# q, k and v computed with features on the partitions, and the rotary rows moved by transfers, in a decoder block on one core

## The chip, the core and the metric

The kernel runs on one core of a Trainium2 chip. The core has TensorE (matrix products, PE in the profile), VectorE (DVE), ScalarE (ACT), GpSimd (POOL) and SyncE (SP). SP, ACT and POOL also issue transfers (DMA), which all run on the core's 16 DMA engines. The engines run side by side and each executes its own instructions in order, waiting on semaphores of the others. The metric is the device time of one execution in microseconds; the median of several runs is compared.

## The reference

One decoder block on x of 1024 tokens and 1024 features, in float32. What bears on the change:

```python
h = _rmsnorm(x, g_mix_pre[l])                       # x * rsqrt(mean(x*x) + eps) * g
proj = einsum('bsd,de->bse', h, w_in[l]) + b_in[l]  # e: 512 pool, 512 q, 128 k, 128 v, 2048 gates
u_pool, q, k, v, gates = split(proj)
q = _partial_rotary(q)    # 8 heads of 64; of each head the first 16 features are turned:
k = _partial_rotary(k)    # 2 heads       t1*cos - t2*sin, t2*cos + t1*sin, with 8 + 8 features
y_attn = _sliding_window_sink_attention(q, k, v, attn_sinks[l])   # blocks of 128 tokens, window 128
```

After that come the gates, the pooling mixer, the output projection, and an MLP of 4096; the change does not touch them.

## The kernel before, in words

**Precision and layout.** Every product is made of three matmuls on a high and a low part of each operand (PASSES: high x high, high x low, low x high). x is loaded transposed (`xt`, features on the partitions), scaled by the gain and split by `scaled` into `xs_[k][th]`: eight slices k of 128 features, two halves th of 512 tokens. The factor of the norm, `r1`, is one number per token: it isn't applied to x but to the results. It comes from `ssq`, the sums of squares of x in rows (`square_row`, ACT), by `rsqrt` (a square root on ACT and small operations on DVE).

**The projection (L180 to L193).** For a block of 128 tokens the piece of x is the stationary operand and the weights move: `mm_q` makes a result of 128 tokens x 512 q features (matmuls of 512 columns), `mm_kv` one of 128 tokens x 256 (k and v). The first loop over k (L216) loads x and the weights and does this for blocks 0 to 3; blocks 4 to 7 are done later. Since tokens are on the partitions of the result, `pre_q` and `pre_kv` close it in one DVE instruction each: times r1 (a per-partition scalar), plus the bias (a row that is broadcast). `rotate` turns the 16 features of all heads (on DVE for block 0, else on GpSimd), and `post_qkv` turns q and k by five transposes on TensorE, since the scores want features on the partitions, and splits them into high and low parts: `qt`, `khi`, `klo`.

**The order.** From L894 on a hand-written program sets the order of TensorE, DVE and ACT; the other queues and, ahead of it, all engines are ordered by the framework. In this program `fill(t)` takes about t us of matmuls from the generator `others`, which yields the projection of the second half, then halves of the gate products. Attention goes block by block: `score_all`, `softmax_max`, `softmax_exp`, `softmax_scale`, `attend_t`, `attend_v`, with a fill between the steps. `make_rb` (L476) writes r1 to DRAM and loads it broadcast over the partitions, `rb`: the gates, whose results have tokens on the free dimension, are multiplied by it later. An accumulator in PSUM is a `bank`: four of tag "mm", two pairs of tag "sc". A tile pool with n buffers makes the n+1st tile of a tag wait until the first is no longer read.

Of the kernel before, what the change touches and what calls it, by code (L numbers as in the profile page):

```python
# [36 lines left out]
C_COS = C_MASK + 2 * P  # L37
C_SIN = C_COS + NT * 8
C_CNT = C_SIN + NT * 8
# [7 lines left out]
V_N = V_ONE + 1  # L47
# [3 lines left out]
def block_kernel(ctx: ExitStack, tc, xt, x, consts, vecs, sinks, b_qkv, g_post, g_mlp, g_mlp_post,  # L51
# [128 lines left out]
    def mm_q(n, k, bq):  # L180
        for j, (xh, h) in enumerate(PASSES):
            pe.matmul(bq, xs_[k][n // 4][:, xh, n % 4 * P:(n % 4 + 1) * P], wq[k][:, h, :],  # L182
                      start=k == 0 and j == 0, stop=k == NK - 1 and j == 2)

    def bkv_of(n):
        return bkv[n // 2 * 2][:, n % 2, :] if n < 4 else bkv[n][:, 0, :]

    def mm_kv(n, k, joint=False):

        for j, (xh, h) in enumerate(PASSES):  # L190
            pe.matmul(bkv_of(n), xs_[k][n // 4][:, xh, n % 4 * P:(n % 4 + 1) * P],  # L191
                      wkv[k // 2][:, h, k % 2, :], start=k == 0 and j == 0 and not (joint and n % 2),
                      stop=k == NK - 1 and j == 2 and not (joint and n % 2 == 0))  # L193

    bq01, bq23 = bank("sc", [2, 512]), bank("sc", [2, 512])
    bq = {0: bq01[:, 0, :], 1: bq01[:, 1, :], 2: bq23[:, 0, :], 3: bq23[:, 1, :]}
    bz = bank("mm")
    bkv = {0: bank("mm", [2, 256]), 2: bank("mm", [2, 256])}
    for j in range(9):
        pe.matmul(bz, zeros[:, :P], zeros, start=j == 0, stop=j == 8)  # L200
    def scaled(t, xs, gk, th, a, b):
        src = xs[:, th * 512 + a:th * 512 + b]
        act.activation(t[:, 0, a:b], src, AF.Identity, scale=gk)
        dve.scalar_tensor_tensor(t[:, 1, a:b], src, gk, f32(t[:, 0, a:b]), ALU.mult, ALU.subtract)


    later = []

    ssq = small()

    def square_row(n):
        t = at(*(("qkv", 3) if n % 2 == 0 else ("s4", 4)), [S])
        nc.sync.dma_start(t, x[n])
        act.activation(t, t, AF.Square, accum_out=ssq[:, n:n + 1])

    for k in range(NK):  # L216
        xs = at("s4", 4, [S])
        ws = stage([768]) if k else ws_first
        if k < 2:
            if k == 0:  # L220
                nc.sync.dma_start(vec, vecs)
            for a, b in ((0, 256), (256, 512)) if k == 0 else ((0, 512),):
                nc.sync.dma_start(xs[:, a:b], xt[k][:, a:b])
            if k:
                nc.sync.dma_start(ws, w_qkv[k])
            else:
                nc.sync.dma_start(ws[:, 512:], w_qkv[k][:, 512:])
            later.append((k, xs))
        else:
            nc.sync.dma_start(xs, xt[k])  # L230
            nc.sync.dma_start(ws, w_qkv[k])
            if k == 2:
                for i, t in later:
                    nc.sync.dma_start(t[:, 512:], xt[i][:, 512:])
        halves_ = [xp.tile([P, 2, 512], F32R, tag="x", name=nm("x")) for _ in range(2)]
        gk = vec[:, V_G + k:V_G + k + 1]
        q = wslot([2, 512]) if k < 6 else ga_.tile([P, 2, 512], F32R, tag="ga", name=nm("wq"))
        if k % 2 == 0:
            wkv.append(ga_.tile([P, 2, 2, 256], F32R, tag="ga", name=nm("wkv")))
        kv = wkv[-1]  # L240
        first = k == 0
        if first:
            split(q[:, 0, :], q[:, 1, :], ws[:, :512], first=dve)
        for a, b in ((0, 256), (256, 512)) if first else ((0, 512),):
            scaled(halves_[0], xs, gk, 0, a, b)
        if not first:
            split(q[:, 0, :], q[:, 1, :], ws[:, :512])
# [2176 lines left out]
```

## Time and profile before

| | |
|---|---|
| time, median of 3 runs | 1087.27 us (1087.07 to 1088.03) |
| the profiled execution's own time | 1087.07 us |
| its span | 1085.3 us |
| TensorE busy | 1076.5 us (99%) |
| DVE / ACT / POOL busy | 892.6 / 635.5 / 102.1 us |
| granted TensorE clock | 0.998 |

A row of the timeline gives the start in us from the span's start, the duration, engine, line, operation, output <- inputs, shapes and the count of instructions merged; in brackets the idle time of the engine ahead of it and what ended that. A row of the chain of waits gives start, length and what ran. A row of the waits reads: engine and line, what it waited for, us in total, times, longest. A row on transfers gives what was written <- read, the issuing queue, the count, KB of one, and the median us from the issue to the landing.

### The profile page before, as it was taken

The page shows a single profiled execution, that of the slowest core. Times are in us where ns is not written, and L with a number is a line of the kernel's source. Part 1 is how long each engine was busy: PE and PEld are TensorE (multiplying, and loading weights), DVE is VectorE, ACT ScalarE, POOL GpSimd, SP SyncE. Part 2 cuts the span into 40 slices and gives each one's busy share as a digit, 9 for nine tenths or more (in the row PEclk, how much of TensorE's full clock was granted, in tenths as well). Part 3 has the DMA queues.
Part 4 walks back from the last instruction along what each step waited for, and adds up shares of the span by engine and source line. Part 5 has one row for each costly group of instructions (what it writes and reads, how often), then busy time and mean ns, then how long its engine had stood idle before and what let it go on. Part 6 is the DMA issues. An engine that isn't in the chain of part 4 may idle for free.

```text
span 1085.3 us, 14915 instructions
## 1 busy us (share of the span) xinstructions
PE 1076.5 (99%) x5355; PEld 907.9 (84%) x5355; DVE 892.6 (82%) x1297; ACT 635.5 (59%) x1058; POOL 102.1 (9%) x174
## 2 busy tenths in 40 slices
PE   9999999999999999999999999999999999999997
PEld 8888888888888888888888888888888898899885
DVE  6688888999787887879979877776757899898997
ACT  6567886466654247587666555555544473275553
POOL 0354311100100012100000000001000000000000
PEclk9999999999999999999999999999999999999999
DMA  9566899679965785822576654656898687469842
GB/s 335 187 188 176 214 248 343 200 240 305 268 212 176 216 203 126 301 83 93 189 256 250 246 203 167 221 184 218 298 385 278 212 273 256 151 183 331 300 132 78
DMA packets 106618, 242.06 MB, mean 223 GB/s; under 512 B 11056, under 2 KB 28592, under 8 KB 106544
## 3 DMA queue, kind: packets, MB, share of 16 engines
q1 hardware_dynamic: 86528, 191.69, 52.1%
q0 software_dynamic: 14112, 29.37, 11.6%
q10 hardware_dynamic: 5904, 20.06, 4.7%
q8 instruction: 42, 0.69, 0.3%
q14 instruction: 32, 0.26, 0.1%
HBM read 166.63 MB, written 73.40 MB: 221 GB/s over the span
## 4 chain that ended last, share of the span: by engine, by line
PE 94%; DVE 2%; ACT 2%; issue 1%; DMA 0%; DVEq 0%; ACTq 0%
PE mm L583 26%; PE at L583 19%; PE at L2129 12%; PE mm L2129 5%; PE mm L1523 5%; PE at L2103 4%; PE mm L2103 4%; PE mm L494 3%; PE sc L182 2%; PE at L1523 2%; PE at L1251 2%; PE mm L191 2%; PE mm L182 2%; PE mm L1251 2%; PE mm L496 1%; PE sc L456 1%
## 5 line engine op out<-in xcount | busy, mean ns | idle before, releaser
L2129 PE MATMUL at<-ar,wh 128*128 128x512 f32 x564 | 134.6, 389 | 0.0
L2129 PEld LDWEIGHTS at<-ar,wh 128*128 128x128 f32 x564 | 105.8, 188 | 22.2 <-DVE ar L104 0.3
L101 ACT CAST wh<-raw 128x1024 fp32r<-128x1024 f32 (+1 forms) x54 | 53.4, 988 | 80.1 <-PE at L2129 52.3
L104 DVE TENSOR_TENSOR wh<-st,wh 128x512 fp32r<-128x512 f32 (+1 forms) x106 | 76.4, 730 | 25.7 <-ACT wh L101 22.1
L583 PE MATMUL mm<-T,wx 128*128 128x512 f32 x375 | 90.6, 389 | 0.0
L104 DVE TENSOR_TENSOR wh<-raw,wh 128x1024 fp32r<-128x1024 f32 (+1 forms) x54 | 61.7, 1142 | 29.9 <-ACT wh L101 29.4
L583 PEld LDWEIGHTS mm<-T,wx 128*128 128x128 f32 x375 | 70.3, 188 | 14.8 <-DVE wx L104 0.2
L101 ACT CAST wh<-st 128x512 fp32r<-128x512 f32 (+2 forms) x105 | 67.6, 653 | 18.8 <-DVE st L539 6.1
L583 PE MATMUL mm<-gr,wh 128*128 128x512 f32 x321 | 77.5, 391 | 0.0
L583 PEld LDWEIGHTS mm<-gr,wh 128*128 128x128 f32 x321 | 59.9, 188 | 12.2
L2129 PE MATMUL mm<-ar,wh 128*128 128x512 f32 x276 | 69.5, 389 | 0.0
L583 PE MATMUL mm<-T,wh 128*128 128x512 f32 x267 | 66.0, 389 | 0.0
L101 ACT CAST ar<-B 128x1024 fp32r<-128x1024 f32 (+2 forms) x59 | 43.0, 757 | 30.7 <-PE mm L2129 14.8
L2129 PEld LDWEIGHTS mm<-ar,wh 128*128 128x128 f32 x276 | 51.8, 188 | 10.8
L583 PE MATMUL at<-gr,wh 128*128 128x512 f32 x243 | 59.0, 389 | 0.0
L583 PE MATMUL mm<-x,wh 128*128 128x512 f32 x240 | 58.8, 394 | 0.0
L583 PEld LDWEIGHTS mm<-T,wh 128*128 128x128 f32 x267 | 50.1, 188 | 10.4
L583 PEld LDWEIGHTS at<-gr,wh 128*128 128x128 f32 x243 | 45.6, 188 | 9.5
L583 PE MATMUL at<-T,wx 128*128 128x512 f32 x213 | 52.2, 389 | 0.0
L583 PEld LDWEIGHTS mm<-x,wh 128*128 128x128 f32 x240 | 44.2, 188 | 9.6 <-ACT f L692 0.2
L104 DVE TENSOR_TENSOR ar<-B,ar 128x1024 fp32r<-128x1024 f32 (+2 forms) x59 | 49.1, 856 | 1.0 <-ACT ar L101 1.0
L2103 PE MATMUL at<-ar,wh 128*128 128x256 f32 x336 | 47.5, 283 | 0.0
(556 smaller groups left out, 2461.0 us busy)
## 6 DMA issues: line engine op xcount, KB each, us to landing
raw<-f_dram SPq DMA_DIRECT2D x40, 512.0 KB, 4.3
B<-in_w_dn_dram SPq DMA_DIRECT2D x32, 512.0 KB, 6.7
st<-in_w_up_dram SPq DMA_DIRECT2D x27, 512.0 KB, 5.2
f_dram<-g SPq DMA_DIRECT2D x21, 512.0 KB, 3.0
wh<-f_dram SPq DMA_DIRECT2D x20, 512.0 KB, 5.1
g<-spill_dram SPq DMA_DIRECT2D x17, 512.0 KB, 5.7
st<-in_w_g_dram SPq DMA_DIRECT2D x16, 512.0 KB, 5.2
f_dram<-g ACTq DMA_DIRECT2D x16, 512.0 KB, 4.1
```

The costliest lines, as they stand in the source:

```text
L101: act.copy(hi, src)
L104: return eng.tensor_tensor(lo, src, f32(hi), ALU.subtract)
L182: pe.matmul(bq, xs_[k][n // 4][:, xh, n % 4 * P:(n % 4 + 1) * P], wq[k][:, h, :], start=k == 0 and j == 0, stop=k == NK - 1 and j == 2)
L191: pe.matmul(bkv_of(n), xs_[k][n // 4][:, xh, n % 4 * P:(n % 4 + 1) * P], wkv[k // 2][:, h, k % 2, :], start=k == 0 and j == 0 and not (joi ...
L456: pe.matmul(yb[:, kv], v[:, c:c + P], p[ph][:, 4 * kv:4 * kv + 4].rearrange("p i q -> p (i q)"), start=j < 2, stop=j >= len(mms) - 2)
L494: pe.matmul(bs[th], whi[:, k, :], rhs(k, hl, th), start=k == 0 and hl == 0, stop=False)
L496: pe.matmul(bs[th], wlo[:, k, :], rhs(k, 0, th), start=False, stop=k == nk - 1)
L583: pe.matmul(b, w[wh][:, kt, :], x_, start=not after and kt == 0 and j == 0, stop=kt == 3 and j == 2, skip_group_check=after)
L1251: pe.matmul(b, w[wh][:, kt, :], xo[xh][:, kt, :], start=not after and kt == 0 and j == 0, stop=kt == 1 and j == 2, skip_group_check=after)
L1523: pe.matmul(bs[t], Am[a][k][ah][:, t * P:(t + 1) * P], Wm[w][k][wh], start=not after and k == 0 and j == 0, stop=k == 3 and j == 2, skip_g ...
L2103: pe.matmul(part[q][:, t, :], o[fs][fh][:, fk, t * P:(t + 1) * P], o[ws][wh][:, wk, :], start=q not in onto and (s_, t, j) == (0, 0, 0), s ...
L2129: pe.matmul(bs[t], fo[fh][:, k2, t * P:(t + 1) * P], wo_[wh][:, k2, :], start=not after and s2 == 0 and k2 == 0 and j == 0, stop=(s2, k2) ...
```

## The change

The weights become the stationary operand, and half of x (512 tokens) moves: `mm_in(f, th, k)` makes a result of 128 features x 512 tokens, for six tiles f of features and two halves th of the tokens. Features are arranged by the host in six tiles: tiles 0 to 3 hold the unturned features of two q heads (48 each) and 32 features of v between them; tiles 4 and 5 hold, in their first 80 partitions, the turned features of all ten heads, each rotary half in the other tile, and in the rest the unturned features of k. So the results already have features on the partitions, and the transposes of q and k go; only v is transposed (`post_v`). What is added:

- The first loop loads and scales only the first half of the tokens; the second half of x is loaded behind the squares of the first four rows. In the first loop matmuls of k = 6 and 7 are done tile by tile, 4 and 5 first.
- `make_rb` is called once for each half of the tokens, from GpSimd's queue, and `close_in` multiplies a tile of results by `rb` (DVE) and adds the bias (ACT, a per-partition scalar).
- `turn` and `turn_end` turn the 80 rows with tables of cos and sin that are loaded (`load_table`), on DVE for the first half, on GpSimd for the second.
- `rows_in`, `keys_rest` and `values_out` move rows between partitions by transfers: turned rows to their place in the tiles of q and k, the unturned rows of k, and the rows of v.
- `split_k` and `split_q` make the high and low parts from SBUF.
- The three fills ahead of the first scores and the softmax, and the places of the later splits, are set anew.

```diff
-    def mm_q(n, k, bq):
-        for j, (xh, h) in enumerate(PASSES):
-            pe.matmul(bq, xs_[k][n // 4][:, xh, n % 4 * P:(n % 4 + 1) * P], wq[k][:, h, :],
...
+    def mm_in(f, th, k, a=0, b=512):
+        for j, (wh, xh) in enumerate(PASSES):
+            pe.matmul(b_in[f, th][:, a:b], w_in_of(f, k, wh), xs_[k][th][:, xh, a:b],
+                      start=k == 0 and j == 0 and a == 0, stop=k == NK - 1 and j == 2)
...
+    def make_rb(th):
+        c, n = slice(th * 512, (th + 1) * 512), slice(4 * th, 4 * th + 4)
+        rsqrt(r1[:, n], ssq[:, n], 4)
+        row = z_dram[0][0][c]
+        nc.gpsimd.dma_start(row.rearrange("(n p) -> p n", p=P), r1[:, n])
+        nc.gpsimd.dma_start(rb[:, c], row.unsqueeze(0).broadcast_to([P, 512]))
...
+        for f in (4, 5, 0, 1, 2, 3):
+            for k in (6, 7):
+                mm_in(f, 0, k)
+        for n in range(4):
+            square_row(n, at("qkv", 3, [S]) if n < 3 else at("s4", 4, [S]))
+        make_rb(0)
+        load_table(0)
+        for k in range(NK):
+            if k % 2 == 0:
+                xs = flat(yy.tile([P, 2, 512], F32, tag="y", name=nm("xs")))
+            nc.sync.dma_start(xs[:, k % 2 * 512:(k % 2 + 1) * 512], xt[k][:, 512:])
+            scaled(k, 1, xs[:, k % 2 * 512:(k % 2 + 1) * 512])
+        for n in range(4, NT):
+            square_row(n, at("s8", 3, [2, 4, P]).rearrange("p a b k -> p (a b k)") if n < 7 else at("s4", 4, [S]))
...
-    def pre_q(n):
-        dve.scalar_tensor_tensor(tf_of(n)[:, :512], bq[n], r1[:, n:n + 1], bq_b[:, :512], ALU.mult, ALU.add)
...
+    def close_in(f, th):
+        raw_in(f, th)
+        t = raw_of(f, th)
+        dve.tensor_tensor(t, b_in.pop((f, th)), rb[:, th * 512:(th + 1) * 512], ALU.mult)
+        act.activation(t, t, AF.Identity, bias=vec[:, V_BQ + f:V_BQ + f + 1])
...
+    def turn(th, eng):
+        t, tab = raw_r[th][:NR], tables.pop(th)
+        turned[th] = [at("s4", 4, [2, 512])[:NR] for _ in range(2)]
+        for i, o in enumerate(turned[th]):
+            eng.tensor_tensor(o, t, tab[:NR, i, :].unsqueeze(1).broadcast_to([NR, 2, 512]), ALU.mult)
+
+    def turn_end(th, eng):
+        t, (a, b) = raw_r[th][:NR], turned.pop(th)
+        eng.tensor_tensor(t[:, 0], a[:, 0], b[:, 1], ALU.subtract)
+        eng.tensor_tensor(t[:, 1], a[:, 1], b[:, 0], ALU.add)
+
+    MOVES = ((0, 0, 16, 56), (1, 0, 8, 48), (1, 8, 16, 72))
+
+    def rows_in(q, th, dst, m):
+        for i, a, b, to in MOVES:
+            q.dma_start(dst[to:to + b - a], raw_r[th][16 * m + a:16 * m + b, i, :])
+
+    def split_k(th):
+        c = slice(th * 512, (th + 1) * 512)
+        split(khi[:, c], klo[:, c], raw_k.pop(th))
...
     def others():
+        for f in (4, 5, 0, 1, 2, 3):
+            b_in[f, 1] = bank("mm")
+            for k in range(NK):
+                mm_in(f, 1, k)
...
+                if k == NK - 1:
+                    close_in(f, 1)
+                    if f == 5:
+                        keys_rest(nc.sync, 1)
+                        turn(1, pool)
+                        turn_end(1, pool)
+                        rows_in(nc.sync, 1, raw_k[1], 4)
+                    elif f < 4:
+                        values_out(nc.sync, 1, f)
+                        rows_in(nc.sync, 1, raw_of(f, 1), f)
+                    if f == 1:
+                        split_k(1)
                 yield 3 * 0.227
...
-        rsqrt(r1, ssq[:, :NT], NT)
-        make_rb()
...
+        close_in(4, 0)
+        close_in(5, 0)
+        turn(0, dve)
+        keys_rest(nc.sync, 0)
+        load_table(1)
+        for m in (0, 1):
+            close_in(m, 0)
+            values_out(nc.scalar, 0, m)
+        make_rb(1)
+        turn_end(0, dve)
+        rows_in(nc.sync, 0, raw_k[0], 4)
+        for m in (2, 3):
+            close_in(m, 0)
+            values_out(nc.scalar, 0, m)
...
-        fill(5.7)
...
+        fill(5.4)
+        split_k(0)
+        split_q(0)
+        fill(3.4)
         score_all(0)
```

**Where the order shows it.** First TensorE ahead of the scores of block 0 (`sc<-klo,qt`). Before, these rows stand there (`mm_529` is the kv result of block 4, `mm_596` the q result of block 5):

```order
L191 MATMUL mm_529<-wkv_365,x_363 128x256 x3
L191 MATMUL mm_529<-wkv_365,x_406 128x256 x3
L182 MATMUL mm_596<-wh_120,x_119 128x512 [waits DVE_49]
L182 MATMUL mm_596<-wh_120,x_119 128x512 x2
L388 MATMUL sc_601<-klo_470,qt_558 128x128 [waits DVE_49]
```

In the changed kernel (`mm_555` is tile 5 of the second half; tile 4 of the second half, `mm_520`, is complete ahead of these rows):

```order
L185 MATMUL mm_555<-x_124,wkv_118 128x512 [waits PE_49]
L185 MATMUL mm_555<-x_124,wkv_118 128x512 x2
L185 MATMUL mm_555<-x_168,wkv_118 128x512 x3
L185 MATMUL mm_555<-x_200,wkv_195 128x512 x3
L185 MATMUL mm_555<-x_230,wkv_195 128x512 x3
L185 MATMUL mm_555<-x_262,wkv_257 128x512 x3
L420 MATMUL sc_572<-klo_457,qt_550 128x128 [waits DVE_49,PE_49,Activation_49]
```

The transposes are gone, and the first scores come behind 24 + 15 matmuls of the second half.

Second, DVE ahead of the splitting of k (`klo`) of block 0. Before, the rows are these, and `r_86` (r1) is what the closing instructions read:

```order
L311 SCALAR_TENSOR_TENSOR qkv_490<-sc_98,r_86,bc_460 128x512
L311 SCALAR_TENSOR_TENSOR tf_492<-sc_99,r_86,bc_460 128x512
L311 SCALAR_TENSOR_TENSOR tf_494<-sc_99,r_86,bc_460 128x512
L104 TENSOR_TENSOR qt_558<-mm_551,qt_558 128x512 [waits Activation_49]
L104 TENSOR_TENSOR klo_470<-mm_552,khi_469 128x128 [waits Activation_49]
```

In the changed kernel they read `rb_all`, and the closing of tile 4 of the second half (`mm_520`) stands ahead of `klo`. Its waits hold DMASW3, the fourth transfer of GpSimd's queue, which is the load of the second half of rb:

```order
L346 TENSOR_TENSOR qkv_460<-s_69_465,s_70_466 80x512
L347 TENSOR_TENSOR qkv_460<-s_69_465,s_70_466 80x512
L332 TENSOR_TENSOR qkv_499<-sc_99,rb_all 128x512 [waits PE_49]
L332 TENSOR_TENSOR qkv_499<-sc_99,rb_all 128x512
L941 TENSOR_SCALAR nsnk<-snk 128x8 [waits DMAHW5_49]
L332 TENSOR_TENSOR qkv_545<-mm_520,rb_all 128x512 [waits DMAHW3_49,DMAHW2_49,DMAHW4_49,DMAHW1_49,DMAHW5_49,DMAHW0_49,DMAHW6_49,DMASW3_49,DMAHW7_49,DVE_49,PE_49]
L103 TENSOR_TENSOR klo_457<-s_71_469,khi_456 128x512 [waits Activation_49]
L103 TENSOR_TENSOR qt_550<-qkv_474,qt_550 128x256 [waits Activation_49]
```

So k and q of the first half are split behind a wait for the factor of the second half.

Third, ACT from the first bias (L333, of tile 4 of the first half, which needs rb of that half) to the square root of the second half (`sm_481<-ssq`, L108):

```order
L333 ACTIVATE qkv_460<-qkv_460,vec 128x512 [waits DVE_49]
L207 ACTIVATE s_60_435,ssq<-s_60_435 128x1024 [waits DMAHW0_49]
L333 ACTIVATE qkv_460<-qkv_460,vec 128x512 [waits DVE_49]
L207 ACTIVATE s_61_438,ssq<-s_61_438 128x1024 [waits DMAHW1_49]
L207 ACTIVATE s_62_441,ssq<-s_62_441 128x1024 [waits DMAHW2_49]
L207 ACTIVATE s_63_444,ssq<-s_63_444 128x1024 [waits DMAHW3_49]
L333 ACTIVATE qkv_474<-qkv_474,vec 128x512 [waits DVE_49]
L362 DMA tv<-qkv_474 32x512 [waits Activation_49]
L333 ACTIVATE qkv_474<-qkv_474,vec 128x512 [waits DVE_49]
L362 DMA tv<-qkv_474 32x512 [waits DMAHW4_49,Activation_49]
L108 ACTIVATE sm_481<-ssq,eps 128x4
```

Before, the eight squares and one square root of all tokens stood together ahead of every closing; now the squares of rows 4 to 7 are behind the first closings.

266 lines of the change are left out of this document (117 added, 149 removed).

## The prediction

> **What bounds the kernel now.** I read the busy times first, then the chain that ended last, then TensorE's own waits, and then the first 70 us (the only stretch that the change touches) instruction by instruction.
>
> ```profile
> PE 1076.5 (99%) x5355; PEld 907.9 (84%) x5355; DVE 892.6 (82%) x1297; ACT 635.5 (59%) x1058; POOL 102.1 (9%) x174
> PE 94%; DVE 2%; ACT 2%; issue 1%; DMA 0%; DVEq 0%; ACTq 0%
> ...
> PE mm L200 <- PEq L2410: 0.8, 1, 0.8
> PE sc L431 <- DVE s L420: 0.2, 1, 0.2
> ```
>
> TensorE works from the first microsecond to the tail and makes up 94% of the chain; in the whole span it waits for others 1.0 us. So a matmul less is time won, and every new microsecond in which TensorE must wait is time lost, one for one. The stretch of the change in the chain of waits:
>
> ```profile
> 0.78 4.18 PE mm L200 x9
> 4.95 3.41 PE sc L182 x12
> ...
> 34.90 2.75 PE sc L182 x12
> 39.08 5.47 PE mm L182 x24
> 45.44 2.51 PE mm L191 x21
> 48.65 1.49 PE sc L388 x24
> ```
>
> A matmul of 512 columns costs 5.47/24 = 0.228 us, one of 256 columns 2.51/21 = 0.1195, and the first k is 3.41 - 2.75 = 0.66 us late. The first scores (L388) start at 48.65, with no gap ahead of them.
>
> **TensorE's work.** The kv matmuls (L191) are 192 of 256 columns, 22.9 us; the change has 96 more of 512 in their place, 21.9: 1.0 saved. The first k's twelve 512-wide ones become 24 of 256: 12 x (0.239 - 0.228) = 0.13 lost. Of 40 transposes (five a block) 8 stay:
>
> ```profile
> 58.43 0.60 PE L344 MATMUL mm<-cst,tf 128*128 128x128 f32 x4
> 58.87 0.27 PE L345 MATMUL mm<-cst,tf 128*128 128x128 f32 x1
> ```
>
> Four take 58.87 - 58.43 = 0.44 from start to start, 0.11 each; 32 fewer save 3.5. In sum TensorE has 4.4 us less to do. That is the whole possible gain.
>
> **What the first scores wait for.** In the kernel before, the factor r1 (one value per token) is a per-partition scalar: once it is in SBUF, the projections are closed. Its copy along the free dimension, rb, is made too, but nobody wants it before the gates. Now that tokens lie on the free dimension, closing a tile needs rb: for each half of the tokens r1 goes to DRAM in elements of 4 bytes and comes back broadcast. This is the same pair of transfers that the profile shows off the path:
>
> ```profile
> 35.84 1.06 ACT L214 ACTIVATE s<-s 128x1024 f32<-128x1024 f32 x1 [0.16 <-DMA s<-in_x_dram]
> 37.01 1.28 ACT L109 ACT_TABLE_LOAD   x1
> 39.48 0.17 DVE L121 TENSOR_TENSOR r<-sm,sm 128x8 f32<-128x8 f32 x1
> 39.68 0.37 SPq L479 DMA_DIRECT2D spill_dram<-r  x1
> 50.03 0.34 SPq L480 DMA_DIRECT2D rb_all<-spill_dram  x1
> ...
> spill_dram<-r SPq DMA_DIRECT2D x1, 4.0 KB, 10.3
> rb_all<-spill_dram SPq DMA_DIRECT2D x1, 512.0 KB, 4.8
> spill_dram<-st SPq DMA_DIRECT2D x8, 256.0 KB, 2.4
> f<-spill_dram POOLq DMA_DIRECT2D x5, 256.0 KB, 3.8
> g<-spill_dram POOLq DMA_DIRECT2D x3, 256.0 KB, 6.2
> ```
>
> 4 KB took 10.3 us to land where 256 KB took 2.4, and the load behind it really waited: it was issued at 50.03. The packet counts of two stretches (40.4 to 41.0 and 41.0 to 41.6) say why it is not the engines' work:
>
> ```profile
> DMA packets 649, 0.00 MB, mean 4 GB/s; under 512 B 649, under 2 KB 649, under 8 KB 649
> ...
> DMA packets 386, 0.00 MB, mean 3 GB/s; under 512 B 386, under 2 KB 386, under 8 KB 386
> ```
>
> The 1024 elements had left by 41.6, and the landing came 8.4 us later: something behind the engines takes about 8 ns for each. The change writes 512 at a time, from GpSimd's queue, whose small writes this trace does not show. Low bound: 2.4, as a plain write. High: 10.3, as now. I take the row it is nearest to, with half of what goes with the count: 2.4 + (10.3 - 2.4)/2 = 6.4. For the load of 256 KB the rows on GpSimd's queue give 3.8 to 6.2; I take 5.0 for the first (the second half of x is still being loaded then) and 3.8 for the second.
>
> **When each happens.** The loads ahead of the last square were 8 x 896 KB + 8 x 512 KB = 11.5 MB before, landing at 35.84 from about 2.5: 0.346 MB/us. Ahead of the fourth square are now 8 x 640 KB + 4 x 512 KB = 7.3 MB: 2.5 + 21.2 = 23.7. From that landing to r1 the kernel before took 39.65 - 35.84 = 3.8, so the first half of r1 is there at 27.5, and rb at R = 27.5 + 6.4 + 5.0 = 38.9. Two of the tiles to be closed will have been done on TensorE since about 33.
>
> The second half's r1 stands behind R, because ACT executes in order: the bias of tile 4 (which needs rb) is ahead of the squares of tokens 4 to 7, and these are ahead of the second square root. Prices:
>
> ```profile
> 27.15 1.34 ACT L203 ACTIVATE x<-s,vec 128x512 fp32r<-128x512 f32 x2
> ...
> 45.91 1.40 DVE L311 SCALAR_TENSOR_TENSOR tf<-sc,r,bc 128x512 f32<-128x512 f32 x2
> 47.22 0.68 DVE L104 TENSOR_TENSOR qt<-mm,qt 128x512 fp32r<-128x512 f32 x1
> 61.73 1.32 DVE L420 TENSOR_TENSOR s<-s,den 128x1024 f32<-128x1024 f32 x1
> ```
>
> Closing tile 4 on DVE 0.65, two x pieces queued behind it 1.3, closing tile 5 0.65, its bias on ACT 0.7: R + 3.3. ACT then has three squares of 1.24 (1.06 and the accumulator's read), to R + 7.0, while DVE turns (two of 1.2) and closes tiles 0 and 1, also to R + 7.0; then two biases (0.67) with a DMA issue of 0.4 behind each, R + 9.1, the root 0.3 and four dependent small operations on DVE 1.2: r1's second half at R + 10.6. Its round trip is 6.4 + 3.8, so all of rb is there at R + 20.8. The rows that are put in place meanwhile (some twenty transfers of 16 to 96 KB, 0.4 us of issue each on SP and ACT, 2 to 3 us to land) leave from R + 11.9 and are there by about R + 19: hidden by that second trip; without that cover they cost what they take after it, up to their own 7 us.
>
> Why should the scores of block 0, which are of the first half, wait for the second half's rb? Because closing tile 4 of the second half is written ahead of the splitting of k and q in DVE's order, and its bias ahead of the casts in ACT's. DVE stands at that instruction, and queued behind it are klo, both pieces of q's low part, presum and the first softmax; PE waits for them at the first scores. After rb: closing 0.65, bias 0.67, the cast of k 0.6, low part of k and the first piece of q 1.0: the scores start at R + 23.7 = 62.6.
>
> TensorE is there much earlier: 4.95 + 0.66 + 24 x 0.1195 + 132 x 0.228 = 38.6 for the first half, and 39 matmuls of the second, 8.9: **47.5**. It stops for 62.6 - 47.5 = **15.1 us**. Bounds: with 2.4 and 3.8 on both trips 27.5 + 6.2 + 10.6 + 6.2 + 2.9 = 53.4, a stop of 5.9; with 10.3 and 6.2 it is 74.0, a stop of 26.5.
>
> After a stop TensorE may start slowly. The nearest row is the span's own start: nine matmuls of 512 columns took 4.18 us, where 9 x 0.228 = 2.05 would do, so 2.1 lost; bounds 0 and 2.1, and I take 2.1, since a stop of 15 us is more like a start than like a gap. [...]
>
> Later only one place worries me. The second half is turned on GpSimd, and its prices there are:
>
> ```profile
> 66.94 0.54 POOL L326 TENSOR_TENSOR rb<-qkv,cst 128x160 f32<-128x160 f32 x1
> 69.01 0.35 POOL L328 TENSOR_TENSOR qkv<-qkv,rb 128x80 f32<-128x80 f32 x1
> 72.95 0.98 POOL L326 TENSOR_TENSOR rb<-qkv,cst 128x160 f32<-128x160 f32 x1
> ```
>
> 0.19 us for 80 elements more: 2.5 for 1024 and 1.3 for 512, 7.6 for the four, and up to 14 where they run as slowly as the 0.98. If T is the start of the first scores, key tile 5 is closed and biased at T + 7, turned at T + 14.6 to 21, in place 3 us later; ACT's cast of those keys is ahead of its copy that frees a bank for the scores of block 2, which TensorE reaches at T + 22.3. With cast and copy (1.6) that is a stop of 0 to 3.3; I take 1.5. DVE's extra work (twelve closings of 0.65, two turns of 1.2, for twelve closings of 0.7 and 0.45) and ACT's twelve biases lie in the stop or beside TensorE's fill work: nothing; without that cover ACT's are 8 us.
>
> **Sum**, against the profiled execution's own 1087.07 us (0.2 from the median 1087.27, so the same): 1087.1 - 4.4 + 15.1 + 2.1 + 1.5 = 1101.4, said as 1101.
>
> **The rivals.** (1) *Small transfers at their floor.* If 512 elements from GpSimd's queue land as fast as the quickest rows of the trace, the trips are short:
>
> ```profile
> out_dram<-xf SPq DMA_DIRECT2D x6, 256.0 KB, 2.1
> st<-wbp_dram SPq DMA_DIRECT2D x8, 256.0 KB, 2.9
> ```
>
> Two trips of 2.1 + 2.9: 27.5 + 5.0 + 10.6 + 5.0 + 2.9 = 51.0, a stop of 3.5, 1086. Against it is the 10.3. [...] (2) *Faster*: rb is never late, as the first half's loads are fewer, and TensorE runs through: 1087.1 - 4.4 = 1082.7. For it speaks that TensorE never waited for x before. It needs both trips together within 47.5 - 27.5 - 10.6 - 2.9 = 6.5 us, four landings of 1.6 where the quickest is 2.1; or r1 some microseconds earlier. (3) *More stops*: the first trip is stretched by the loads of x (10.3 instead of 6.4 for the write), and the turn on GpSimd runs at its slow price: 1101.4 + 3.9 + 1.2 (6.2 for that load, too) + 1.8 = 1108.
>
> **How the numbers follow.** Forecast 0.67, with a range of its own of 1094 to 1107; rival 1 0.10, rival 2 0.06, rival 3 0.17. The bounds of the stop without any other loss give 1087.1 - 4.4 + 5.9 = 1088.6, and with all 1087.1 - 4.4 + 26.5 + 2.1 + 3.3 = 1114.6; the range is 1088 to 1114. What a measurement can tell is 0.2%, 2.2 us: rival 2 and part of rival 1 are faster (0.08), most of the rest of rival 1 is the same (0.07), the others are slower (0.85).
>
> **What would show it.** In the changed kernel's profile: a stop of TensorE of about 15 us ahead of the first scores (L420), near 47; DVE's L332 waiting about ten us for the load of rb_all; two writes of r, 2 KB each, at 5 to 8 us; TensorE's work 4 us less. Wrong would be writes of r at 2 to 3 us, r1's first half well before 25, or no stop at the scores. If the stop is there and the time is still near 1087, work that I take as fixed was saved later.

## The result, and the profile after

The changed kernel takes **1141.54 us** (median of four runs, 1141.02 to 1143.64) beside 1087.17 for the kernel before in the same session: a ratio of 1.0503, 95% interval 1.0490 to 1.0516. It is slower, as forecast, but by 54 us and not by 14, and the time lies above the forecast's range (1088 to 1114). The profiled execution took 1141.17 us, its span is 1139.0, the granted clock 0.981 (0.998 before).

TensorE's busy time and its waits in the changed kernel (engine and line, what it waited for, us in total, times, longest):

```profile
PE 1096.9 (96%) x5239; PEld 905.4 (79%) x5239; DVE 899.3 (79%) x1301; ACT 644.5 (57%) x1081; POOL 97.2 (9%) x146
```
```profile
PE sc L420 <- DVE klo L103: 21.7, 1, 21.7
PE mm L185 <- DVE x L201: 7.2, 1, 7.2
PE sc L420 <- ACT yt L490: 2.5, 2, 2.2
PE sc L463 <- DVE s L429: 1.0, 2, 0.5
PE sc L463 <- DVE s L452: 1.0, 1, 1.0
PE mm L196 <- PEq L2457: 0.8, 1, 0.8
```

The stop ahead of the first scores is there (L420), and a second one that the prediction did not have: the second half's x pieces (L201) stand on DVE behind the closing of tile 4, which waits for rb. The chain of waits and DVE's two waits at the closing (L332):

```profile
31.85 12.32 DMA spill_dram<-r
...
44.47 4.58 DMA rb_all<-spill_dram
...
52.51 3.12 ACT s L207 x6
...
62.17 6.63 DMA tv<-qkv
68.82 4.90 DMA qkv<-qkv
...
74.43 1.98 DMA qkv<-qkv
...
79.51 2.85 PE sc L420 x24
...
82.76 6.54 PE mm L185 x21
```
```profile
49.14 0.69 DVE L332 TENSOR_TENSOR qkv<-mm,rb_all 128x512 f32<-128x512 f32 x1 [13.64 <-DMA rb_all<-spill_dram]
...
76.68 0.69 DVE L332 TENSOR_TENSOR qkv<-mm,rb_all 128x512 f32<-128x512 f32 x1 [14.63 <-DMA qkv<-qkv]
```

rb's first half was there at 49.1. What ended DVE's second wait is not the second half of rb but the moved rows (`qkv<-qkv`): they have to be out of a buffer that the second half takes over. The two writes of r1 on GpSimd's queue, of 2 KB each, landed 12.3 and 8.1 us after their issue:

```profile
spill_dram<-r POOLq DMA_DIRECT2D x1, 2.0 KB, 12.3
...
spill_dram<-r POOLq DMA_DIRECT2D x1, 2.0 KB, 8.1
```

The table by stretches gives for each the length, the busy time of PE, PEld (weight loads), DVE, ACT and POOL with counts, the granted clock, the share of the DMA engines' time, and GB/s. It shows a half clock up to about 86, seven us after TensorE had gone back to work (0.68 is 6.4 us at a half), and once more behind a stop of only 2.2 us at 108 to 110:

```profile
70.00:80.00 10.00, 0.49 (x4) 0.52 (x6) 2.02 (x5) 3.33 (x6) 0.00 (x0) 0.50 0.23 57
80.00:90.00 10.00, 10.00 (x56) 8.26 (x58) 7.01 (x13) 3.93 (x13) 2.98 (x3) 0.68 0.25 81
...
108.00:110.00 2.00, 0.04 (x2) 0.04 (x2) 0.96 (x2) 2.00 (x4) 0.00 (x0) 1.00 0.51 158
110.00:112.00 2.00, 2.00 (x14) 1.68 (x15) 1.66 (x3) 0.98 (x2) 0.00 (x0) 0.57 0.34 64
```

And a loss that no wait shows. From about 200 us on both kernels run the same code, and yet the distance between them grows: the gates begin at 162.35 before and 201.82 after (39.5 later), the MLP's 384 matmuls end at 865.95 and 918.75 (52.8 later). The granted clock is 1.0 in both. The groups of matmuls say where; a row ends with the count, the busy us, the mean ns of one, and the idle time ahead:

```profile
L2167 PE MATMUL at<-ar,wh 128*128 128x512 f32 x564 | 138.8, 396 | 0.0
...
L607 PE MATMUL mm<-T,wx 128*128 128x512 f32 x375 | 90.7, 389 | 0.0
```
```profile
L2129 PE MATMUL at<-ar,wh 128*128 128x512 f32 x564 | 134.6, 389 | 0.0
...
L583 PE MATMUL mm<-T,wx 128*128 128x512 f32 x375 | 90.6, 389 | 0.0
```

The second fence is the kernel before. The same 564 matmuls take 396 ns instead of 389, while others kept their 389.

### The profile page after: what moved, and what is told of

The parts are those of the page before. It is cut to its first block, busy times and chain, and to the rows that moved or that the text cites. A ratio compares the mean times of both kernels' runs of the same rounds, so it can differ in the third digit from the quotient of the medians.

```text
span 1139.0 us, 14784 instructions
## 1 busy us (share of the span) xinstructions
PE 1096.9 (96%) x5239; PEld 905.4 (79%) x5239; DVE 899.3 (79%) x1301; ACT 644.5 (57%) x1081; POOL 97.2 (9%) x146
## 4 chain that ended last, share of the span: by engine, by line
PE 85%; DMA 5%; ACT 4%; DVE 4%; issue 1%; SPq 0%; ACTq 0%; DVEq 0%
PE mm L607 25%; PE at L607 18%; PE at L2167 12%; PE mm L2167 5%; PE mm L1561 5%; PE at L2141 3%; PE mm L2141 3%; PE mm L518 3%; PE at L1561 2%; PE at L1289 2%; PE mm L1289 1%; PE mm L520 1%; DMA spill_dram<-r 1%; PE sc L420 1%; DMA s<-in_x_dram 1%
## 5 line engine op out<-in xcount | busy, mean ns | idle before, releaser
L2167 PE MATMUL at<-ar,wh 128*128 128x512 f32 x564 | 138.8, 396 | 0.0
L607 PEld LDWEIGHTS mm<-T,wx 128*128 128x128 f32 x375 | 70.4, 188 | 14.9
L607 PE MATMUL at<-gr,wh 128*128 128x512 f32 x243 | 60.8, 396 | 0.0
L100 ACT CAST ar<-B 128x1024 fp32r<-128x1024 f32 (+2 forms) x59 | 43.0, 756 | 30.0 <-PE mm L2167 15.2
L607 PEld LDWEIGHTS mm<-T,wh 128*128 128x128 f32 x267 | 50.2, 188 | 10.9
L607 PE MATMUL at<-ar,wh 128*128 128x512 f32 x192 | 47.5, 396 | 0.0
```

The lines of the kernel that those rows point to most:

```text
L100: act.copy(hi, src)
L607: pe.matmul(b, w[wh][:, kt, :], x_, start=not after and kt == 0 and j == 0, stop=kt == 3 and j == 2, skip_group_check=after)
L2167: pe.matmul(bs[t], fo[fh][:, k2, t * P:(t + 1) * P], wo_[wh][:, k2, :], start=not after and s2 == 0 and k2 == 0 and j == 0, stop=(s2, k2) ...
```

## The experiments

All times stand beside a kernel before of 1087.1 to 1087.9 us in the same session. Line numbers of the variants are one to some ten lines higher than in the changed kernel.

### Where the operands lie in SBUF

The slow groups are those with an operand in the buffers `ga` or `g` (names `ar`, `gr`). The change dropped the tables of cos and sin and a tile of `rotate`, so these buffers begin elsewhere. First bytes of the buffers modulo 256, as the built programs place them:

```
               weights (wh)   ga, g (ar, gr)   x, wx, yp, most of T
before             224             224             224
after              224             128             224
```

**a_shift96**, the changed kernel:

```diff
     pad = sp.tile([P, 32], F32, name="pad", bufs=1)
+    dve.memset(sp.tile([P, 24], F32, name="gap", bufs=1), 0.0)
```

> The changed kernel with one unused tile of 96 bytes per partition ahead of the big buffers and nothing else. In the changed kernel some tiles were dropped and made smaller, so the buffers that hold operands of the later stages (tags ga and g) begin at an address that is 0 modulo 128, where it was 96 before; the weights (tag wh) and x stay at 96. Theory: the place of the operands in SBUF costs the matmuls their 2 to 3% (the MLP's 384 matmuls 87.04 us before, 89.96 after). Then the last 940 us get some 14 us back: 1127, and those 384 matmuls take 87. Rival: the slower matmuls are an after-effect of the stops (a clock or power state); then nothing moves: 1141, 90.

Measured: 1127.76 us (1126.84 to 1130.9), 13.8 less; the MLP's 384 matmuls take 87.04 us again, and the 564 above 389 ns.

**b_shift32**, **b_shift64**, **b_shift128**: the kernel before with such a tile of 32, 64, 128 bytes. **b_all0**: 32 bytes ahead of all big buffers and 96 on the right side, where x lies.

> The kernel before with an unused tile of 32 bytes per partition, which puts the buffers ga and g at 0 modulo 128, as in the changed kernel, and nothing else. By the theory of the place it loses what the changed kernel lost after 200 us, 14 to 16 us: about 1102, and the MLP's 384 matmuls take 90. By the rival: 1087, 87.

> The kernel before with an unused tile of 64 bytes, so that ga and g begin at 32 modulo 128, which is 32 modulo 64 as before. If what counts is the place modulo 64, nothing moves: 1087, 87. If it is the place modulo 128 against that of the other operand (96), it loses as the shift by 32 does: 1102, 90. If the stops are the cause: 1087.

> The kernel before with 32 bytes ahead of all big buffers on the left and 96 on the right, so that every operand begins at 0 modulo 128. If what costs is that the two operands lie differently, nothing is lost: 1087, 87. If an operand at 0 modulo 64 is slow by itself, the loss is that of the shift by 32 or larger, since x and the weights have it too: 1102 to 1115, 90. If the stops are the cause: 1087.

> The kernel before with an unused tile of 128 bytes ahead of the buffers ga and g. In all runs so far the matmuls ran at 389 ns where both operands begin at the same place modulo 256, and at 391 to 396 where they do not. If 256 is the measure, this run is slow as the shift by 32 is: 1097 to 1102, ar against wh 391 to 396. If 128 is the measure, nothing moves: 1087, 389.

Measured: 1101.33 us for 32 bytes (ratio 1.0131, 1.0116 to 1.0146), 1096.67 for 64 (1.0085, 1.0070 to 1.0100), 1101.97 for 128 (one run), 1097.81 for b_all0 (1.0098, 1.0081 to 1.0115). So an unused tile of 32 bytes makes the kernel before 14 us slower. Which groups, in three fences (32 bytes; 128 bytes; b_all0):

```profile
L2130 PE MATMUL at<-ar,wh 128*128 128x512 f32 x564 | 138.2, 395 | 0.0
```
```profile
L2130 PE MATMUL at<-ar,wh 128*128 128x512 f32 x564 | 138.1, 395 | 0.0
```
```profile
L2132 PE MATMUL at<-ar,wh 128*128 128x512 f32 x564 | 134.6, 389 | 0.0
...
L586 PE MATMUL at<-x,wh 128*128 128x512 f32 x96 | 23.6, 394 | 0.0
```

In b_all0 `ar` begins at the very byte at which it is slow with 32 bytes (50432), and is fast, because the weights now begin at 0 modulo 256 too; x, at 128, is slow instead. So the place of one operand does not count, but that of the two against each other: the large groups at 389 ns have both at the same place modulo 256, and a difference of 32, 64 or 128 costs 2 to 7 ns of each matmul. Modulo 64 and modulo 128 are excluded as the measure by the 64 and the 128 bytes. More than 256 is not needed: in the kernel before, `wh` begins at 24032, `ar` at 50400 and `yp` at 147424, an odd and an even multiple of 256 away, and both pairs run at 389. Equal places are not the whole of it: behind 200 us, 36 of that kernel's 44 groups of this shape run at 389, the others at 390 to 399. Why the chip does so stays open. Of the change's 54 us, 14 are this. It comes with the tiles that were dropped, not with the layout of q, k and v or its stops.

### What the first scores wait for

**a_order**, on a_shift96:

```diff
-        fill(5.4)
         split_k(0)
         split_q(0)
-        fill(3.4)
+        fill(8.8)
```

> The changed kernel with the 96 bytes (1127.8), and the splitting of k and q of the first half moved ahead of the first fill, so that on DVE and ACT it no longer stands behind the closing of tile 4 of the second half, which reads the second half of rb. The prediction's step: this order alone makes the first scores wait for the second half's factor; then they start when the first half is ready and most of the stop of 22.6 us goes: 1110 or less. Rival, from the trace of the changed kernel: the last to land ahead of the scores are the moved rows of q of the first half (77.0; rb's second half is there at 73.8), which the scores need in any order; then only the closing and bias that stood ahead go (0.7 + 0.7): 1126.

Measured: 1127.89 us (1125.75 to 1129.87): nothing. The order that the prediction blamed is there, but it isn't what ends last.

**a_norows**, on a_order: the twelve `rows_in` of q's first half left out.

> The kernel of a_order (splits ahead of the fill, 1127.9, no gain), with the twelve transfers left out that put the turned rows of q's first half in place (the output lacks them; the rows of k and v are still moved). If the row moves are what the first scores wait for, the splitting of k and q can start when the rows of k are there, some 4 us after the end of the turn at 60.7, and the scores 2 to 3 us later, at 67 instead of 80: 1115. If they wait for something else (the second half's factor, the biases), the scores stay at 77 or later: 1125 or more.

Measured: 1120.29 us (1118.24 to 1120.94), 7.6 less. The stop fell from the first row (a_order) to the second (a_norows), and the third, from the chain of a_norows, says what holds it now:

```profile
PE sc L421 <- DVE klo L103: 21.0, 1, 21.0
```
```profile
PE sc L421 <- DVE klo L103: 13.2, 1, 13.2
```
```profile
62.64 8.00 DMA s<-qkv
```

The moved rows of q were last, as the rival said. But the rows of k, 64 KB in three transfers, now take 8.0 us by themselves, not the 4 I had put down. They land at 70.6, and the second write of r1, issued at 60.9, lands 9.3 us later, at 70.2: the rows wait about as long as that write is under way.

**a_rbpe**, on a_shift96, takes both trips away:

```diff
-        row = z_dram[0][0][c]
-        nc.gpsimd.dma_start(row.rearrange("(n p) -> p n", p=P), r1[:, n])
-        nc.gpsimd.dma_start(rb[:, c], row.unsqueeze(0).broadcast_to([P, 512]))
...
+        diag = tv[:, c].rearrange("p (n q) -> p n q", q=P)
+        dve.tensor_tensor(diag, ident.unsqueeze(1).broadcast_to([P, 4, P]),
+                          r1[:, n].unsqueeze(2).broadcast_to([P, 4, P]), ALU.mult)
+        b = bank("mm")
+        pe.matmul(b, ones, tv[:, c], start=True, stop=True)
+        act.copy(rb[:, c], b)
...
```

> The changed kernel, with both round trips of r1 through DRAM taken out: the factor is put on a diagonal (DVE, 128 x 512) and TensorE multiplies it by a matrix of ones, which puts r1 along the free dimension in all partitions; ACT copies that to rb. Two f32 matmuls of 512 columns more, the constants are loaded ahead of the second half of x, the big buffers lie as with the 96 bytes (1127.8). rb's first half should then be there at about 34.5 instead of 49.1, and r1's second half 10.4 later, at 45. If the trips are the whole cause, as predicted, and the moved rows take 7 us, the first scores start at about 55, TensorE stops some 4 us there and nowhere before: 1101. If the moves take what they took in the changed kernel (16 us from the end of the turn at 46), they become the bound: scores at 64, a stop of 11 to 13: 1109. If the trips are not the cause: 1127.

Measured: **1108.05 us** (1103.71 to 1110.27; ratio 1.0174, 1.0147 to 1.0202), 19.7 less than a_shift96. rb's first half is copied at 35.2. What is left:

```profile
PE mm L224 <- DVE tv L222: 6.5, 1, 6.5
PE sc L428 <- DVE klo L103: 3.3, 1, 3.3
PE sc L428 <- ACT yt L498: 3.2, 3, 2.3
```

The first is the multiplication for the second half, which stands too early in TensorE's order; the second is the stop at the scores. All its waits but the one at the start come to 18.0 us; one minus the clock, by what TensorE was busy in each stretch of 10 us, to 6.5. Less the 2.6 of saved work that are left (4.4, less an estimated 1.8 for the two f32 matmuls), that is 21.9 of the 23.2 us by which the profiled run lies above the kernel before.

From its chain, the first transfer of the values that ends a wait, and the last moved row:

```profile
49.90 1.99 DMA tv<-qkv
...
55.71 1.99 DMA qkv<-qkv
```

The turn ends at 48.5 and the last moved row lands at 57.7: 9.2 us. In the changed kernel the same moves take from 60.8 to 76.4, 15.6 us. Of the 6.4 more, 4.6 are in the transfer of the values (6.63 instead of 1.99), which lands 0.7 behind the write of r1 that was issued ahead of it; the rest comes behind it, while the second half of rb is loaded. Both are gone in a_rbpe, so this run alone doesn't tell them apart; in a_norows the rows of k were held before that load was issued, at 70.4.

### What a small write costs, and whom

**a_writes**, on a_shift96: five more writes on GpSimd's queue.

```diff
+    def write_rows(t):
+        nc.gpsimd.dma_start(scrap[:512].rearrange("(n p) -> n p", p=P), t)
+
+    def write_elements(t, n):
+        nc.gpsimd.dma_start(scrap[:n * P].rearrange("(n p) -> p n", p=P), t)
+
+    write_rows(gap[:4, :P])
+    write_elements(gap[:, P:P + 1], 1)
+    write_elements(gap[:, P:P + 4], 4)
...
+        write_rows(rb[:4, 512:640])
+        write_elements(r1[:, 4:5], 1)
```

> The changed kernel with five more writes on GpSimd's queue, each behind the landing of the one ahead, to a row of DRAM that nobody reads: while the loads run, 4 rows of 512 bytes, 128 elements of 4 bytes, 512 elements of 4 bytes; and behind the second load of rb, in a quiet stretch, the 4 rows and 128 elements again. By the prediction's step (a fixed price, and a part that goes with the number of elements) in the quiet: rows 2.4, 128 elements 3.4, and 512, which the kernel itself writes, 6.4 (measured: 8.0 to 8.5). If the loads stretch a write as they did for the first factor (11.8 to 12.6): 512 elements 10 or more, and the rows, being four packets, at most 4.

Measured, in the order of issue: the rows, 128 elements, 512 elements, all under the loads; then rows and 128 elements again in the quiet:

```profile
spill_dram<-gap POOLq DMA_DIRECT2D x1, 2.0 KB, 2.7
...
spill_dram<-gap POOLq DMA_DIRECT2D x1, 0.5 KB, 10.5
...
spill_dram<-gap POOLq DMA_DIRECT2D x1, 2.0 KB, 10.1
...
spill_dram<-rb_all POOLq DMA_DIRECT2D x1, 2.0 KB, 1.8
...
spill_dram<-r POOLq DMA_DIRECT2D x1, 0.5 KB, 8.2
```

The number of elements is not the price: 128 cost 8.2 us, 512 cost 8.1 to 9.3 behind the loads, 1024 cost 10.3 in the kernel before. That it is elements of 4 bytes is: the same 2 KB in rows of 512 bytes take 1.8. And others pay too. Two stretches of a_writes, the first with a write of elements under way, the second with none (last columns: share of the DMA engines' time, GB/s), and the first of them in a_shift96:

```profile
20.00:24.00 4.00, 4.00 (x19) 3.30 (x19) 0.97 (x2) 0.18 (x1) 0.00 (x0) 1.00 1.13 68
...
28.00:32.00 4.00, 4.00 (x19) 3.34 (x18) 1.54 (x3) 1.94 (x4) 0.00 (x0) 1.00 1.04 414
```
```profile
20.00:24.00 4.00, 4.00 (x20) 3.30 (x19) 1.86 (x4) 2.81 (x6) 0.00 (x0) 1.00 1.02 408
```

The engines are busy and move 68 GB/s instead of 408. It isn't so for the whole of a write: in stretches of 1 us the loads run on at first, and then stay at 34 to 105 GB/s (from 11 to 17, and from 20 to 27; the two writes were issued at 4.4 and 15.2). Two such writes during the loads made r1's own write start at 42.1 instead of 31.1, and the one run came out at 1137.1 us, 9.3 more. So an element write holds up loads, as the rows of k in a_norows and the values in the changed kernel were held up beside one.

**a_rows**, on a_shift96 (constants loaded early as in a_rbpe): `pe.transpose(b[:4, :P], r1[:, n], ident)`, a copy on ACT, and a write of 4 rows.

> The changed kernel with the 96 bytes (1127.8), and r1 written to DRAM in rows: TensorE transposes the 128 x 4 values to 4 x 128, ACT copies them, and GpSimd's queue writes 4 rows of 512 bytes in place of 512 elements; the broadcast load stays. In a_writes such rows landed in 1.8 to 2.7 us, the elements in 8.2 to 10.9. If the 4-byte elements are the price, each write falls by 6 to 9 us: rb's first half at 42 instead of 49, r1's second half at 52, the scores at 63 to 65 (moved rows last): 1110 to 1113. If any write of that queue pays it, nothing moves: 1127.

Measured: 1124.99 us (1123.01 to 1126.71): only 2.8 less, where I had expected 15 or more. The price of the write fell (6.2 in place of 12.4 under the loads, and 1.6 in place of 8.1 behind them), but the scores start at 75.9, only 3.9 earlier:

```profile
PE mm L221 <- DVE r L120: 13.4, 1, 13.4
PE sc L428 <- DVE klo L103: 12.4, 1, 12.4
```

The second transpose stands in TensorE's order ahead of 18 matmuls and waits there for r1, and ACT's copy of its result stands behind ACT's six moved rows: it ran at 67.1, though r1 was there at 56.7. rb's first half came at 46.2 (49.1). The moved rows, with no write under way, take 9.1 us here (the turn ends at 57.9, the last lands at 67.0), as in a_rbpe. So this run shows the price of the elements, what it does to the moved rows, and that a cheap trip in a bad place of an in-order queue wins nothing; it says nothing on what a well placed one would give.

### The cold clock

**a_warm**, **a_warm2**, **a_warm3**, on a_shift96: matmuls of zeros added to the accumulation of tile 5 of the second half: 85 ahead of k = 7 in a_warm, 85 ahead of k = 4 in a_warm2, 100 there in a_warm3, which the diff shows.

```diff
+                if f == 5 and k == 4:
+                    for j in range(100):
+                        pe.matmul(b_in[f, 1], zeros[:, :P], zeros, start=False, stop=False)
```

> The changed kernel with the 96 bytes, and 85 matmuls of zeros (19.3 us) added to the accumulation of tile 5 of the second half, ahead of its last k, so that TensorE is busy in the stop. They end ahead of the first scores, so the stop itself stays. If a cold clock costs what the trace shows (the granted clock is a half from 62 to 86, and the scores' matmuls run at half rate to 86.4), it comes back: the clock stays 1.0 from 56 on, and 3.5 us are won: 1124. If ACT and DVE set the pace there anyhow, nothing: 1128.

> As a_warm, with the 85 matmuls of zeros ahead of k = 4 of tile 5 of the second half, which TensorE reaches before the first scores (in a_warm they stood ahead of k = 7, which it reaches only behind them, so they cost their own 18.6 us). They fill the stop from about 57 to 77; the scores still start at 80. If the cold clock costs, 3 to 3.5 us come back: 1124; if DVE and ACT set the pace anyhow, nothing: 1128.

> As a_warm2 (1128.1), with 100 instead of 85 matmuls of zeros, so that they reach the first scores (a_warm2's ended 3.7 us ahead of them, and the clock fell to a half again in that gap: 0.73 from 80 to 90). If the half clock costs what the trace shows behind the stop, about 3.5 us come back: 1124.5. If DVE and ACT set the pace there, nothing: 1128.

Measured: 1149.63, 1128.1 and 1127.1 us. In a_warm the filler stood behind the first scores, so it only added time (21.9 us, for 85 matmuls that are an estimated 19.3). In a_warm2 it ended 3.7 us early, and the clock fell again in that gap. In a_warm3 it reached the scores (the rows are a_warm2 and a_warm3):

```profile
80.00:90.00 10.00, 10.00 (x64) 8.46 (x66) 7.23 (x14) 3.98 (x14) 3.26 (x3) 0.73 0.27 88
```
```profile
80.00:90.00 10.00, 10.00 (x63) 8.10 (x62) 7.54 (x13) 6.95 (x27) 5.87 (x4) 1.00 0.48 149
```

The gates then start at 199.3 instead of 202.5: 3.2 us won, as expected. In the whole time the gain is 0.7, within the 4 us by which the runs of these variants differ; in the profiled run 2.6 us were lost again between 600 and 620, where TensorE waited for a cast of weights. So the size of the loss is shown where it arises, and not in the whole.

### The layout without its stops

**a_best** and **a_best2**, on a_rbpe: the turn of the first half ahead of the second square root, rows moved from three queues (in a_best2 from SP's and GpSimd's), a fourth buffer for the raw results, more matmuls ahead of the first scores; in a_best2 the second half is turned on DVE too. In a_best the values leave behind the rows that take their place, so v holds turned rows there; number and size of the transfers are those of a_best2.

> The layout of the change with every cause taken out that the runs have shown: buffers at the same place modulo 256, rb made by TensorE, DVE's turn of the first half not behind the second square root, the second half's factor needed only behind the split of k and q, rows moved from three queues, a fourth buffer for the raw results, and 14.3 us of the second half's matmuls ahead of the first scores instead of 8.8. If stops, clock and matmul pitch were the whole loss, what is left is the forecast without stops, 1087.1 - 4.4, plus two f32 matmuls (1.8) and some 3 us of the small stops in the softmax: 1087 to 1090. If the layout costs something else that I have not seen: 1095 or more.

> As a_best, with what its trace showed mended: the second half is turned on DVE, behind the first block's softmax (GpSimd's turn made two copies on DVE take 2.8 us each instead of 0.73); the row moves of the second half leave from GpSimd's queue, so that no load of weights stands behind them on SP's; the values go out ahead of the rows that take their place (in a_best behind them, so that its values were overwritten); 12.2 us of matmuls ahead of the first scores. TensorE then arrives at 52, the moved rows land at about 54 and the scores start at 56: a stop of 4, a cold clock of 3 behind it, 3 us of small stops: 1087.1 - 4.4 + 1.8 + 10 = 1094. If the layout costs something unseen: 1105 or more.

Measured: 1118.01 (1115.9 to 1118.95) and 1115.83 us (1114.34 to 1117.12), both slower than a_rbpe. The stop ahead of the first scores is gone in a_best, and 3.3 + 0.9 us in a_best2 (ahead of the multiplication for rb, and of the scores), but new ones came. In a_best (DVE, then GpSimd):

```profile
59.20 5.68 DVE L441 COPY_PREDICATED s<-cst,pad 128x512 f32<-128x512 uint32 x2
```
```profile
58.78 5.52 POOL L354 TENSOR_TENSOR s<-qkv,s 80x1024 f32<-80x1024 f32 x2 [2.24 <-ACT qkv L345]
```

Two copies that take 0.73 us each elsewhere (a_rbpe, at 63.2) end at 64.9, just behind the first two instructions of GpSimd's turn (64.3), and a wait of 4.3 us at the scores of block 1 follows. The two rows show them side by side; why the copies are slow then, no run here shows. In a_best2 waits of 0.3 to 3.3 us remain, 18 us in sum; the longest, and two stretches:

```profile
PE mm L228 <- DVE tv L222: 3.3, 1, 3.3
PE mm L619 <- ACT wh L100: 2.0, 1, 2.0
```
```profile
90.00:100.00 10.00, 8.53 (x39) 6.98 (x39) 6.68 (x9) 6.13 (x23) 5.09 (x11) 0.73 0.82 211
100.00:110.00 10.00, 7.64 (x20) 5.78 (x21) 5.46 (x11) 3.25 (x7) 1.63 (x4) 0.66 0.76 217
```

The clock is below 1.0 in seven of the ten stretches of 10 us between 50 and 150; one minus it, by what TensorE was busy in each, comes to some 11 us. With the 18, and less the 2.6 of saved work that are left, that makes 26 of the 30 us by which the profiled run lies above the kernel before. The work that I had put beside TensorE's at no price (closings, biases, splits on DVE and ACT) is what several of these waits end with. So the layout with no stops was not reached: whether it can come down to 1087 stays open. No version tried beats the kernel before.

## Why the prediction was right and wrong

The direction was right, and so was the first half of its reason: once rb is on the path, TensorE stops ahead of the first scores, and the 4.4 us of saved work don't pay for that (a_rbpe, without the trips, is 19.7 us faster). The terms of the sum, against the changed kernel's profiled execution:

| term | predicted | measured |
|---|---|---|
| TensorE's work | -4.4 | not by itself; 116 matmuls fewer, as counted (5239 for 5355) |
| stops ahead of the first scores | 15.1, at most 26.5 | 28.9 (21.7 and 7.2) |
| half clock behind stops | 2.1 | 7.5 |
| other stops | 1.5 | 5.7 |
| matmuls slower by their operands' place | not seen | 13.8 (changed kernel less a_shift96) |
| sum | 14.3 | 51.5 of 54.1 with the -4.4 as predicted; 2.6 not assigned |

The half clock is counted from the rows above and one of before: 20 matmuls between 50 and 60 take 7.24 us instead of 4.56, the scores 2.85 instead of 1.49, the next 21 matmuls 6.54 instead of 4.8, and the four us from 110 run at 0.57 and 0.58: 2.7 + 1.4 + 1.7 + 1.7.

**The step that failed first** is the price of the write, "half of what goes with the count". Nothing goes with the count between 128 and 512 elements; the write costs 8 to 9 us behind the loads and 10 to 13 under them (13.4 in a_norows), where I took 6.4 and at most 10.3. I had read "about 8 ns for each" out of the count of packets, but 128 elements take as long as 512. The first trip took 12.3 + 4.6 for 11.4. r1 itself was there at 31.5 for 27.5, since the last square's row landed at 27.8: the loads ran at 0.29 MB/us and not at 0.346. So R was 49.1, not 38.9. The step from R to the second r1 held: R + 10.9 for R + 10.6.

**"Hidden by that second trip"** was wrong for a reason that I had not considered. I priced the moved rows at 7 us, and they take 9.2 and 9.1 in a_rbpe and a_rows, where no element write is under way. In the changed kernel the second write is issued just ahead of them, and they land at R + 27.3, past the second half of rb (R + 24.4). A transfer of 2 KB was the expensive one, and I had not asked what it does to the others. The scores start at R + 30.4, not R + 23.7.

**What the change does elsewhere** was put at nothing: the prediction calls the first 70 us "the only stretch that the change touches", and so priced every matmul as before. The dropped tiles moved the operands of the later stages, which cost 13.8 us, as much as the stops came out too long. Without it the kernel would still take 1127.8, above the range.

**The order on DVE and ACT** was named as the reason that block 0 waits. It is in the program, and without it nothing changes (a_order): two waits lie side by side, and the longer is the rows.

**The second stop, 7.2 us**, came of my own figure for TensorE's arrival: I let it run 39 matmuls of the second half, though eight x pieces are scaled on DVE, two of them behind the closing of tile 4 ("two x pieces queued behind it 1.3" stands in the prediction). That TensorE waits for these two was not asked.

**The clock.** The 2.1 us for one cold start is near what each of them costs (1.7 to 3.1); there were three. The shortest stop with a drop behind it in the changed kernel's profile is one of 2.25 us with 0.5 more shortly ahead of it (0.57 from 110 to 112); in a_warm3 the clock stayed at 1.00 between 600 and 620, with a stop of 2.2 us in that stretch. So I would count a stop of over 2 us as one that may have a cold start behind it.

**GpSimd's turn** took 5.10 and 2.57 us for the four instructions, 7.7 in all (7.6 predicted), and a stop of 2.2 us, within the 0 to 3.3 of that term, stands at the named copy on ACT. But its cause was another, so that was luck. The last transfer of those keys' rows was issued at 96.6, and ACT's cast of them came only at 108.4, behind a bias that waited for DVE:

```profile
107.77 0.72 ACT L333 ACTIVATE q<-q,vec 128x512 f32<-128x512 f32 x1 [2.40 <-DVE q L332]
108.40 0.60 ACT L100 CAST khi<-s 128x512 fp32r<-128x512 f32 x1
```

That is the closing of a tile of q behind DVE's softmax: work that the prediction put beside TensorE's at nothing. With the rows in place by an estimated 99 (some 2 us after their last issue, as other moves) and TensorE there at 107.7, the turn alone would have cost nothing.

**The rivals.** Rival 1's price for the write, 2.1, is near what rows of 512 bytes take (1.6 and 1.8 us behind the loads), and not what elements take (8.1 to 12.3 us for the changed kernel's two writes), so its condition did not hold; rival 2, no stop, did not come either. Rival 3 had the first write right, stretched by the loads, but the slow turn did not come, and it too has nothing for the moved rows or the operands. For this write, pieces of 4 and 512 bytes are the only sizes tried: where between them the price ends, and why the elements pay it, no run here shows.

## What to carry to other kernels

Ask of each small transfer what its contiguous piece is, not how many bytes it has: a write of 4-byte elements took 8 us or more whatever their number, cut loads to a sixth for some six us (68 GB/s instead of 408 in four of them), and held small moves between partitions for as long as it was under way (6.63 us instead of 1.99 for the values in the changed kernel, 8.0 for the rows of k in a_norows). When a change adds or drops a tile, compare the first bytes of the matmul operands before and after; here 32 unused bytes were worth 14 us, more than the whole gain that the change was after. And once TensorE has no stop at all, a new stop of 2 us can be paid nearly twice, by its cold clock (2.2 and 1.7 here).

## What the runs showed of the hardware that I had not expected

- Most matmuls of 512 columns took 389 ns each (226.7 from start to start in the MLP) where both operands begin at the same place modulo 256 bytes in SBUF, and 391 to 396 (up to 234 from start to start) elsewhere: 9.5 to 15 us of 1087.
- A write of 128 elements of 4 bytes to DRAM took 8.2 us in the quiet and 10.5 under loads; one of 4 rows of 512 bytes took 1.6 and 1.8, and 2.7 and 6.2 under loads. With elements under way, loads fell from 408 to 68 GB/s in a stretch of 4 us, with the DMA engines' share at 1.13.
- The granted clock fell to a half behind a stop of 2.25 us (0.57 and 0.58 in the two stretches of 2 us from 110; not behind one of 2.2 us in a_warm3, 1.00 from 600 to 620) and came back after 4 to 7 us of work (1.00 from 114, and from about 86 behind the stop of 21.7).
- Two copies on DVE took 2.8 us each instead of 0.73 while GpSimd worked on operands in SBUF.
